# The first pair of an output projection: its products reordered, its carries bare, a store and the gate rows moved to other places

## The chip, the cores and the metric

The kernel runs on one core of a Trainium2 chip. The time is that of one execution on the device in microseconds (us); of several executions the median is given. A profile is one execution of its own, recorded by the hardware. The engines are TensorE (PE in the profile; its weight loads are PEld), VectorE (DVE), ScalarE (ACT), GpSimd (POOL) and SyncE (SP). Each takes its instructions in a fixed order. SP, ACT and POOL also issue transfers (DMA), each through a queue of its own.

## The reference

One layer of a streaming encoder over 2048 prompt frames and 32 frames of a running stream, each of width 1024. Cut to what matters here:

```python
proj = rmsnorm(h, g_mix) @ w_in                  # 1024 -> 3072, six parts
yA   = b * causal_conv3(c * h_in) * silu(zA)     # 512 wide
yB   = pooled_mix(v) * silu(zB)                  # 512 wide
h    = h + concat([yA, yB]) @ w_out              # the stage that is changed
gate = sigmoid(rmsnorm(h, g_ple) @ w_ple_gate)
h    = h + (p @ w_ple) * gate                    # p @ w_ple: the "embedding"
out  = rmsnorm(h, g_final)
```

All is float32. Two states of the mixers are outputs too.

## The kernel before

A float32 product is made of three TensorE products: each operand is split (`split`, L76) into a high part, rounded by ScalarE, and a low part, the difference, by VectorE; high by high, high by low and low by high are added up in PSUM. A tile of frames has 128 rows; `tiles` numbers 16 of them and a last one of 32.

The stages follow each other: the input projection and the mixers, in blocks of 416 columns, which write their result y to memory (`y_d`); the embedding of the first three tiles (`EARLY`, run at the end of that stage by `embedding[1](c)`); the w_out stage; the embedding of the rest; the gate stage; the final norm. The embedding's results go to memory (`e_d`) and are read in the gate stage.

The w_out stage takes the tiles in pairs. For a pair, the left matrix has two halves in rows (the two tiles) and two in columns (the two halves of y), and so has w_out; `seven` (L200) makes the block product from seven half products in place of eight (a Strassen-Winograd scheme). Sums and differences of blocks of y are made by `frame_parts` (L167): S1 to S4 beside the plain 11, 12 and 22. Those of w_out are T1 to T4; T1, T2, T3 and T4 of w_out are ready when the stage begins, 11 is too (`layout(["11"])`, from `tops`). The blocks 21 and 22 come from the bottom half of w_out, four row blocks of 512 KB (`bots`, tile `wo_q`), whose loads SP issues at the start of the stage; `rest` (L1162) splits them: ScalarE's casts make the high parts (`wo_c` for 21, `wo_d` for 22), VectorE's subtractions the low ones (`wo_d`; three tiles, d0 to d2, have this name in the profile).

A product of seven has four steps of k, with three matmuls each: twelve matmuls. Three PSUM banks take them: X (`x_o`), Y (`y_o`) and Z (`z_o`). X goes on to add to what it holds; so a `carry` first copies what it holds so far, and the next product into X waits for that copy. `carry` and `out` come from `h_ops` (L1093): a carry adds the rows of h that the result is added to (`x`) while it copies, on VectorE; a bare one is a plain copy on ScalarE, and VectorE adds it to the rows of `x` later.

The first pair (i = 0) has an order of its own (`t1_first`): S1·T1 into Z, with a bare carry; 11·11 into X, carry; S2·T2 into X, carry; S3·T3 into X, out; 12·21 into Y, out (`late`); S4·22 into Z, out; 22·T4 into X, out. The other pairs start with 11·11 and have S1·T1 between S2·T2 and S3·T3. `between` holds steps that are called between the products.

w_ple_gate, scaled by g_ple, is prepared in this stage too: `scale_gate(k)` (L1131) loads 128 rows through POOL's queue into two tiles `gs`; the function that it returns scales them on ScalarE and stores them to `g_d` through ScalarE's queue. One such block is loaded ahead of the first pair; after each pair it is scaled and stored, and the next is loaded.

The order on each engine is not that of the source: a planner goes over the instructions of a stage and gives each engine a fixed list, keeping what depends on each other in order. A tile of a ring waits for the last reader of the tile that had its place; so tiles of the w_out stage also wait for work and transfers of the stage before, whose places they take.

Of the kernel before, what the change touches and what calls it, by code (L numbers as in the profile page):

```python
# [15 lines left out]
P = 128  # L16
# [18 lines left out]
def trunk(ctx, tc, x_p, x_s, c_conv, c_pool, p_p, p_s, g_mix, w_in, conv_w, conv_b, pool_w,  # L35
# [63 lines left out]
    def embed(todo, wp, ring, queue=nc.sync):  # L99

        got = {}

        def prep(c):
            if c in got or c >= len(todo):
                return
            i = todo[c]
            r, n = tiles[i]  # L110
            if c % 4 == 0:
                pt = ring("p", i)
                m = min(4, len(todo) - c)
                full = [j for j in todo[c:c + m] if j < NT - 1]
                if full:
                    nc.sync.dma_start(pt.rearrange("p (a d) -> p a d", a=4)[:, :len(full)],
                                      p_p[r:r + len(full) * P].rearrange("(a p) d -> p a d", p=P))
                if len(full) < m:
                    nc.sync.dma_start(pt[:DEC, len(full) * PLE:(len(full) + 1) * PLE], p_s)
                got["p"] = pt  # L120
            pt = got["p"][:, (c % 4) * PLE:(c % 4 + 1) * PLE]
            pps = ring("pps", i)
            ptp = tbank(f"ptp_{i}")
            for k in range(2):
                nc.tensor.transpose(ptp[:, k * P:k * P + n], pt[:n, k * P:(k + 1) * P], ident[:n, :n])
            v = ptp.rearrange("p (k t) -> p k t", k=4)[:, :2, :n]
            split(pps[:, 0, :, :n], pps[:, 1, :, :n], v)
            got[c] = pps

        def run(c):  # L130
            i = todo[c]
            r, n = tiles[i]
            prep(c)
            prep(c + 1)
            prep(c + 2)
            pps = got[c]
            o = ring("out", i)
            for nh in range(2):
                cs = slice(nh * NH, nh * NH + NH)
                ps = bank(f"e_{i}_{nh}")  # L140
                for k in range(2):
                    for q, (a, b) in enumerate(((0, 0), (0, 1), (1, 0))):
                        nc.tensor.matmul(ps[:n], pps[:, a, k, :n], wp[k][b][:, cs],  # L143
                                         start=k + q == 0, stop=k == 1 and q == 2)
                nc.scalar.copy(o[:n, cs], ps[:n])
            queue.dma_start(e_d[r:r + n], o[:n])

        return prep, run

    def product(ps, lhs, w, n, start):  # L150

        for k in range(KH):
            for q, (a, b) in enumerate(((0, 0), (0, 1), (1, 0))):
                nc.tensor.matmul(ps[:n], lhs[:, k, a, :n], w[b][:, k], start=start and k + q == 0,  # L154
                                 stop=k == KH - 1 and q == 2, skip_group_check=True)

# [10 lines left out]
    def frame_parts(cmb, tmp, name, a11, a12, a21, a22, t1_first=False):  # L167
# [15 lines left out]
        s1 = comb("S1", a21, a22, ALU.add)  # L183
        if t1_first:
            put("S1", s1)
        put("11", a11)
        s2 = comb("S2", s1, a11, ALU.subtract)
        put("S2", s2)
        if not t1_first:
            put("S1", s1)  # L190
        put("S3", comb("S3", a11, a21, ALU.subtract))

        def more():
            put("12", a12)
            put("S4", comb("S4", a12, s2, ALU.subtract))
            return put("22", a22)

        return A, more

    def seven(name, A, W, carry, out, between={}, late=False, t1_first=False):  # L200

        step = lambda c: between[c]() if c in between else None
        X, Y, Z = (bank(f"{c}_{name}") for c in "xyz")

        def lower():
            product(Z, A["S1"], W["T1"], P, True)  # L210
            return carry(Z, (1, 1))

        if t1_first:
            c3 = lower()
        product(X, A["11"], W["11"], P, True)
        c1 = carry(X, (0, 0))
        step(1)

        def upper():
            product(Y, A["12"], W["21"], P, True)  # L220
            out(Y, c1, (0, 0))

        if not late:
            upper()
        step(2)
        product(X, A["S2"], W["T2"], P, False)
        c2 = carry(X, (0, 1))
        step(3)
        if not t1_first:
# [68 lines left out]
    with ExitStack() as s1:  # L298
# [771 lines left out]
                    early_sums(j)  # L1070

        for c in range(EARLY):
            embedding[1](c)


    with ExitStack() as s2:
# [13 lines left out]
        def half_of(x, at, n=P):  # L1090
            return x[at[0]][:n, at[1] * NH:at[1] * NH + NH]

        def h_ops(x, n, name, bare=None):  # L1093


            def carry(ps, at):
                t = st.tile([P, NH], F32, tag="t", name=f"c_{name}_{at[0]}{at[1]}")
                if at == bare:
                    nc.scalar.copy(t[:n], ps[:n])
                    return t  # L1100
                nc.vector.tensor_tensor(t[:n], ps[:n], half_of(x, at, n), op=ALU.add)  # L1101
                return t

            def out(ps, c, at):
                t = half_of(x, at, n)
                if at == bare:
# [10 lines left out]

        def prep_h(i):
            lo, hi = load_y(i, 2 * P) if i else first_y
            S[i], more = frame_parts(cmb, ss, f"y{i}", lo[:, :, :P], hi[:, :, :P], lo[:, :, P:], hi[:, :, P:], i == 0)  # L1120
            return more

        def short(name, parts, n):
# [246 lines left out]
```

## Time and profile before

| | us |
|---|---|
| median of three executions | 961.4 (960.34 to 961.96) |
| the profiled execution | 960.0 |
| its span, first to last instruction | 958.2 |
| TensorE busy in the span | 930.1 (97%) |
| VectorE, ScalarE, POOL busy | 711.9, 478.0, 133.4 |
| mean clock granted to TensorE, of 1 | 0.993 |
| first pair of the w_out stage, first matmul | 562.44 |
| second pair, first matmul | 586.04 |

The profile's lines give, for an instruction or a group: start, length, engine, line of the kernel, operation, the tile written and the tiles read, shape and count; in brackets the engine's idle time before it and what ended that time (its releaser, inferred). "ACTq", "POOLq" and "SPq" are the issuing of transfers by these engines. The chain that ended last is followed back from the last instruction to whatever released each step; an instruction off that chain could have been later at no cost. Windows are stretches of the span, with the busy time and number of instructions of PE, PEld, DVE, ACT and POOL in turn, then the granted clock of TensorE as a share of the full one, the busy share of the 16 DMA engines, and GB/s.

### The profile page before, as it was taken

The page shows a single profiled execution, that of the slowest core. Times are in us where ns is not written, and L with a number is a line of the kernel's source. Part 1 is how long each engine was busy: PE and PEld are TensorE (multiplying, and loading weights), DVE is VectorE, ACT ScalarE, POOL GpSimd, SP SyncE. Part 2 cuts the span into 40 slices and gives each one's busy share as a digit, 9 for nine tenths or more (in the row PEclk, how much of TensorE's full clock was granted, in tenths as well). Part 3 has the DMA queues.
Part 4 walks back from the last instruction along what each step waited for, and adds up shares of the span by engine and source line. Part 5 has one row for each costly group of instructions (what it writes and reads, how often), then busy time and mean ns, then how long its engine had stood idle before and what let it go on. Part 6 is the DMA issues. An engine that isn't in the chain of part 4 may idle for free.

```text
span 958.2 us, 13167 instructions
## 1 busy us (share of the span) xinstructions
PE 930.1 (97%) x4631; PEld 833.8 (87%) x4631; DVE 711.9 (74%) x1199; ACT 478.0 (50%) x883; POOL 133.4 (14%) x258
## 2 busy tenths in 40 slices
PE   7999999899999999999999989999999999999996
PEld 5999999898999999999999967888886778888883
DVE  6797987989577778585767768656645777898874
ACT  6554564644445554444544455343335775556553
POOL 3112232221001110000000011112110001112112
PEclk9999999999999999999999999999999999999998
DMA  8437696496955557337665297677676784656641
GB/s 260 123 91 216 196 282 218 153 285 218 418 155 153 152 167 212 94 114 262 189 178 171 93 285 234 193 232 228 200 197 207 259 287 133 236 188 231 226 146 49
DMA packets 132415, 190.05 MB, mean 198 GB/s; under 512 B 11708, under 2 KB 101052, under 8 KB 131069
## 3 DMA queue, kind: packets, MB, share of 16 engines
q1 hardware_dynamic: 114909, 133.67, 45.0%
q0 software_dynamic: 14704, 49.78, 15.8%
q10 hardware_dynamic: 2736, 5.77, 2.0%
q8 instruction: 36, 0.59, 0.3%
q14 instruction: 30, 0.25, 0.1%
HBM read 129.06 MB, written 60.10 MB: 197 GB/s over the span
## 4 chain that ended last, share of the span: by engine, by line
PE 69%; DMA 7%; DVE 3%; ACT 2%; issue 1%; POOL 0%; POOLq 0%; SPq 0%; ACTq 0%; DVEq 0%
PE x_g L154 9%; PE x_o L154 8%; PE x_zab L539 5%; PE z_g L154 5%; PE z_o L154 4%; PE x_ch L539 4%; PE x_zbv L539 4%; PE z_zab L539 2%; PE z_ch L539 2%; PE y_g L154 2%; DMA wg_r<-g_d 2%; PE z_zbv L539 2%; PE y_o L154 2%; PE b L539 2%; PE v L539 2%; PE zb L539 2%
## 5 line engine op out<-in xcount | busy, mean ns | idle before, releaser
L143 PE MATMUL e<-wq,pps 128*128 128x512 f32 (+1 forms) x168 | 41.8, 399 | 0.6 <-ACT pps L77 0.6
L77 ACT CAST y_S<-y_fS 128x512 fp32r<-128x512 f32 x32 | 19.6, 621 | 41.2 <-PE x_o L154 19.0
L539 PE MATMUL x_zab<-B,w_zab_S 128*128 128x416 f32 x168 | 35.9, 363 | 2.6 <-ACT V L834 1.9
L539 PE MATMUL z_ch<-B,w_ch_S 128*128 128x416 f32 x168 | 35.7, 363 | 2.6 <-ACT U L834 2.6
L154 PE MATMUL x_o<-wo_b,y_S 128*128 128x512 f32 x128 | 35.7, 391 | 0.9 <-DVE c_o L1101 0.9
L154 PE MATMUL x_g<-wg_b,g_S 128*128 128x512 f32 x128 | 36.3, 391 | 0.0
L143 PEld LDWEIGHTS e<-wq,pps 128*128 128x128 f32 (+1 forms) x168 | 29.5, 182 | 7.6 <-ACT pps L77 0.8
L374 DVE SCALAR_TENSOR_TENSOR xt<-xt,rstd_x,g_bc 128x1024 f32<-128x1024 f32 (+2 forms) x18 | 23.1, 1282 | 17.3 <-POOL rstd_x L73 16.2
L539 PEld LDWEIGHTS x_zab<-B,w_zab_S 128*128 128x128 f32 x168 | 32.3, 194 | 3.7 <-ACT V L834 2.2
L539 PEld LDWEIGHTS z_ch<-B,w_ch_S 128*128 128x128 f32 x168 | 32.5, 196 | 3.4 <-ACT U L834 3.0
L539 PE MATMUL z_zbv<-B,w_zbv_S 128*128 128x416 f32 x168 | 34.2, 352 | 0.0
L539 PE MATMUL z_zab<-B,w_zab_S 128*128 128x416 f32 x168 | 34.2, 352 | 0.0
L539 PE MATMUL x_zbv<-B,w_zbv_S 128*128 128x416 f32 x168 | 34.1, 351 | 0.0
L539 PE MATMUL x_ch<-B,w_ch_S 128*128 128x416 f32 x168 | 34.0, 351 | 0.0
L539 PEld LDWEIGHTS z_zab<-B,w_zab_S 128*128 128x128 f32 x168 | 31.7, 189 | 0.4
L1101 DVE TENSOR_TENSOR c_o<-x_o,x 128x512 f32<-128x512 f32 x16 | 11.1, 692 | 28.0 <-PE x_o L154 28.0
L539 PEld LDWEIGHTS x_ch<-B,w_ch_S 128*128 128x128 f32 x168 | 31.4, 188 | 0.3
L539 PEld LDWEIGHTS x_zbv<-B,w_zbv_S 128*128 128x128 f32 x168 | 31.3, 188 | 0.3
L539 PEld LDWEIGHTS z_zbv<-B,w_zbv_S 128*128 128x128 f32 x168 | 31.3, 188 | 0.4
L69 POOL TENSOR_SCALAR ms_f<-ssq_f 128x1 f32<-128x1 f32 x16 | 7.4, 462 | 169.8 <-ACT junk L88 169.6
L1268 DVE SCALAR_TENSOR_TENSOR h<-h,rstd_f,g_bc 128x1024 f32<-128x1024 f32 x16 | 20.6, 1284 | 12.4 <-POOL rstd_f L73 12.3
L154 PEld LDWEIGHTS x_o<-wo_b,y_S 128*128 128x128 f32 x128 | 24.0, 188 | 6.0 <-ACT y L77 1.3
(534 smaller groups left out, 2662.5 us busy)
## 6 DMA issues: line engine op xcount, KB each, us to landing
y<-y_d SPq DMA_DIRECT2D x16, 512.0 KB, 7.7
x<-in_x_prompt_dram SPq DMA_DIRECT2D x16, 512.0 KB, 7.4
h_d<-x SPq DMA_DIRECT2D x16, 512.0 KB, 2.9
h<-h_d SPq DMA_DIRECT2D x16, 512.0 KB, 3.5
e<-e_d SPq DMA_DIRECT2D x16, 512.0 KB, 5.8
out_dram<-h POOLq DMA_DIRECT2D x16, 512.0 KB, 3.1
xt<-in_x_prompt_dram SPq DMA_DIRECT2D x15, 512.0 KB, 12.4
e_d<-eout SPq DMA_DIRECT2D x13, 512.0 KB, 3.4
```

Of the source, the lines that this page charges most:

```text
L69: nc.gpsimd.tensor_scalar(ms[:n], ssq[:n], scalar1=1.0 / D, scalar2=EPS, op0=ALU.mult, op1=ALU.add)
L77: ins = nc.scalar.copy(hi, src)
L143: nc.tensor.matmul(ps[:n], pps[:, a, k, :n], wp[k][b][:, cs], start=k + q == 0, stop=k == 1 and q == 2)
L154: nc.tensor.matmul(ps[:n], lhs[:, k, a, :n], w[b][:, k], start=start and k + q == 0, stop=k == KH - 1 and q == 2, skip_group_check=True)
L374: nc.vector.scalar_tensor_tensor(xt[:n], xt[:n], r[:n], g_bc[:n], op0=ALU.mult, op1=ALU.mult)
L539: nc.tensor.matmul(ps[:, :NB], lhs[:, k, x], b[:, k, y], start=start and k + q == 0, stop=stop and k == KH - 1 and q == 2, skip_group_chec ...
L1101: nc.vector.tensor_tensor(t[:n], ps[:n], half_of(x, at, n), op=ALU.add)
L1268: nc.vector.scalar_tensor_tensor(h[:n], h[:n], rf[:n], g_bc[:n], op0=ALU.mult, op1=ALU.mult)
```

## The change

Six edits, five of them in or around the first pair.

- The last of the three early embedding tiles: its second half is copied from PSUM by VectorE instead of ScalarE, and its store is issued by POOL instead of ScalarE.
- The first pair no longer starts with S1·T1 (`t1_first` goes). It starts with 11·11; S1·T1 is cut into two halves of two k steps (six matmuls); the first half stands behind 11·11 and the second behind S2·T2 (`in_parts`).
- All three carries of the first pair are bare.
- In three products of the first pair the order of the matmuls within the product is by parts, with k inside: 11·11 takes high by high, high by low (of the weights), low by high; 12·21 and S4·22 take high by high, low (of the frames) by high, high by low (of the weights). Before, and in all other products, k is outside.
- `frame_parts` makes the high and low parts of 11 and S2 ahead of S1 for every pair.
- The gate rows: the first block is loaded behind the first pair in the source; `next_gate` scales what was loaded and loads the next block. It is called after each pair and once more within the second pair.

```diff
-        def run(c):
+        def run(c, last=False):
...
-                nc.scalar.copy(o[:n, cs], ps[:n])
-            queue.dma_start(e_d[r:r + n], o[:n])
+                (nc.vector.tensor_copy if last and nh else nc.scalar.copy)(o[:n, cs], ps[:n])
+            (nc.gpsimd if last else queue).dma_start(e_d[r:r + n], o[:n])
...
-    def product(ps, lhs, w, n, start):
-        for k in range(KH):
-            for q, (a, b) in enumerate(((0, 0), (0, 1), (1, 0))):
+    FINE = (0, 0), (0, 1), (1, 0)
+    def product(ps, lhs, w, n, start, ks=range(KH), order=None):
+        if order is not None:
+            steps = [(k, *p) for p in order for k in ks]
+            for i, (k, a, b) in enumerate(steps):
+                nc.tensor.matmul(ps[:n], lhs[:, k, a, :n], w[b][:, k], start=start and i == 0, stop=i == len(steps) - 1,
+                                 skip_group_check=True)
+            return
+        for k in ks:
+            for q, (a, b) in enumerate(FINE):
...
-    def seven(name, A, W, carry, out, between={}, late=False, t1_first=False):
+    def seven(name, A, W, carry, out, between={}, late=False, in_parts=False):
+        frames_late, weights_late = (FINE, FINE[::2] + FINE[1:2]) if in_parts else (None, None)
-        def lower():
-            product(Z, A["S1"], W["T1"], P, True)
-            return carry(Z, (1, 1))
-        if t1_first:
-            c3 = lower()
-        product(X, A["11"], W["11"], P, True)
+        def lower(*parts):
+            for ks in parts:
+                product(Z, A["S1"], W["T1"], P, ks.start == 0, ks)
+            return carry(Z, (1, 1)) if ks.stop == KH else None
+        parts = range(KH // 2), range(KH // 2, KH)
+        product(X, A["11"], W["11"], P, True, order=frames_late)
...
-            product(Y, A["12"], W["21"], P, True)
+            product(Y, A["12"], W["21"], P, True, order=weights_late)
...
+        if in_parts:
+            lower(parts[0])
         step(2)
         product(X, A["S2"], W["T2"], P, False)
         c2 = carry(X, (0, 1))
         step(3)
-        if not t1_first:
-            c3 = lower()
+        c3 = lower(parts[1]) if in_parts else lower(range(KH))
...
-        product(Z, A["S4"], W["22"], P, False)
+        product(Z, A["S4"], W["22"], P, False, order=weights_late)
...
-            embedding[1](c)
+            embedding[1](c, c == EARLY - 1)
...
-                if at == bare:
+                if bare and at != (1, 0):
...
-        rest_gate = scale_gate(0)
+        gate_rows = iter(range(KC))
+        waiting = []
+        def next_gate():
+            for rest_gate in waiting:
+                rest_gate()
+            waiting[:] = [scale_gate(k) for k in [next(gate_rows, None)] if k is not None]
...
-            seven(f"o{i}", S.pop(i), W, *h_ops(x, P, f"o{i}", None if i else (1, 1)), {1: rest} if i == 0 else {}, True, i == 0)
+            seven(f"o{i}", S.pop(i), W, *h_ops(x, P, f"o{i}", i == 0), {0: {1: rest}, 2: {3: next_gate}}.get(i, {}), True, i == 0)
...
-            rest_gate()
-            if i + 2 < NT - 1:
-                rest_gate = scale_gate(i // 2 + 1)
+            next_gate()
```

More of the change, by code (lines that the diff above doesn't have):

```diff
@@ L165, in weight_sums, with frame_parts @@
             split(W[q][0][:, k], W[q][1][:, k], t)
-    def frame_parts(cmb, tmp, name, a11, a12, a21, a22, t1_first=False):
+    def frame_parts(cmb, tmp, name, a11, a12, a21, a22):
         A = {}
@@ L183, in frame_parts @@
         s1 = comb("S1", a21, a22, ALU.add)
-        if t1_first:
-            put("S1", s1)
         put("11", a11)
@@ L188, in frame_parts @@
         put("S2", s2)
-        if not t1_first:
-            put("S1", s1)
+        put("S1", s1)
         put("S3", comb("S3", a11, a21, ALU.subtract))
@@ L198, in frame_parts @@
         return A, more
-    def seven(name, A, W, carry, out, between={}, late=False, t1_first=False):
+    def seven(name, A, W, carry, out, between={}, late=False, in_parts=False):
         step = lambda c: between[c]() if c in between else None
+        frames_late, weights_late = (FINE, FINE[::2] + FINE[1:2]) if in_parts else (None, None)
         X, Y, Z = (bank(f"{c}_{name}") for c in "xyz")
-        def lower():
-            product(Z, A["S1"], W["T1"], P, True)
-            return carry(Z, (1, 1))
-        if t1_first:
-            c3 = lower()
-        product(X, A["11"], W["11"], P, True)
+        def lower(*parts):
[4 more added lines that the diff above has]
+        product(X, A["11"], W["11"], P, True, order=frames_late)
         c1 = carry(X, (0, 0))
@@ L228, in seven @@
         step(3)
-        if not t1_first:
-            c3 = lower()
+        c3 = lower(parts[1]) if in_parts else lower(range(KH))
         step(4)
@@ L1091, in half_of, with h_ops @@
             return x[at[0]][:n, at[1] * NH:at[1] * NH + NH]
-        def h_ops(x, n, name, bare=None):
+        def h_ops(x, n, name, bare=False):
             def carry(ps, at):
                 t = st.tile([P, NH], F32, tag="t", name=f"c_{name}_{at[0]}{at[1]}")
-                if at == bare:
+                if bare and at != (1, 0):
                     nc.scalar.copy(t[:n], ps[:n])
@@ L1105, in out @@
                 t = half_of(x, at, n)
-                if at == bare:
+                if bare and at != (1, 0):
                     nc.vector.tensor_tensor(t, t, c[:n], op=ALU.add)
@@ L1119, in prep_h @@
             lo, hi = load_y(i, 2 * P) if i else first_y
-            S[i], more = frame_parts(cmb, ss, f"y{i}", lo[:, :, :P], hi[:, :, :P], lo[:, :, P:], hi[:, :, P:], i == 0)
+            S[i], more = frame_parts(cmb, ss, f"y{i}", lo[:, :, :P], hi[:, :, :P], lo[:, :, P:], hi[:, :, P:])
             return more
```

## The prediction

> **What bounds the kernel now.** I read the page first, then the chain that ended last, TensorE's waits around the first w_out pair, the timelines of its engines there, and last the granted clock. The page's first part and the chain (start, length, what):
>
> ```profile
> PE 930.1 (97%) x4631; PEld 833.8 (87%) x4631; DVE 711.9 (74%) x1199; ACT 478.0 (50%) x883; POOL 133.4 (14%) x258
> ```
>
> ```profile
> 555.87 7.08 DMA y<-y_d
> 562.97 15.63 DMA wo_q<-in_w_out_dram
> 580.75 2.73 PE z_o L154 x12
> 583.48 5.44 PE x_o L154 x24
> ```
>
> TensorE is the bound (97%), but not here: before 580.75 the chain runs through a load, the fourth bottom row block of w_out, issued at 562.97 when a y load had landed. The pair's products ahead of y_o are off the chain. One matmul takes 5.44/24 = 0.227 us of TensorE's time. What TensorE waits for between 540 and 590 us (sum, times, longest):
>
> ```profile
> PE x_o L154 <- DVE c_o L1101: 1.8, 2, 0.9
> PE z_o L154 <- ACT y_S L77: 1.7, 1, 1.7
> PE y_o L154 <- ACT wo_c L77: 0.8, 1, 0.8
> PE y_o L154 <- DVE wo_d L78: 0.2, 1, 0.2
> ```
>
> 4.5 us stand idle. The first two lines are what the change goes for; only the last two are on the chain. TensorE's timeline (start, length, instruction, idle before):
>
> ```profile
> 552.08 8.67 PE L143 MATMUL e<-wp,pps 128*128 128x512 f32 x36
> 562.44 3.31 PE L154 MATMUL z_o<-wo_a,y_S 128*128 128x512 f32 x12 [1.69 <-ACT y_S L77]
> ...
> 573.19 2.96 PE L154 MATMUL x_o<-wo_b,y_S 128*128 128x512 f32 x12 [0.88 <-DVE c_o L1101]
> 576.00 0.39 PE L154 MATMUL y_o<-wo_c,y 128*128 128x512 f32 x1
> ...
> 579.29 0.49 PE L154 MATMUL y_o<-wo_c,y 128*128 128x512 f32 x1 [0.84 <-ACT wo_c L77]
> ...
> 580.35 0.40 PE L154 MATMUL y_o<-wo_c,y 128*128 128x512 f32 x1
> 580.59 2.89 PE L154 MATMUL z_o<-wo_d,y_S 128*128 128x512 f32 x12
> ...
> 586.04 2.88 PE L154 MATMUL x_o<-wo_c,y 128*128 128x512 f32 x12
> ```
>
> And ScalarE's, where the three wo_c casts end their wait on a load:
>
> ```profile
> 559.38 0.59 ACT L145 COPY eout<-e 128x512 f32<-128x512 f32 x1 [0.82 <-PE e L143]
> ...
> 561.40 0.33 ACTq L146 DMA_DIRECT2D e_d<-eout  x1
> 561.77 0.62 ACT L77 CAST y_S<-y_fS 128x512 fp32r<-128x512 f32 x1 [0.40 <-ACT eout L145]
> ...
> 574.69 0.62 ACT L77 CAST wo_c<-wo_q 128x512 fp32r<-128x512 f32 x1 [0.62 <-DMA wo_q<-in_w_out_dram]
> ...
> 576.32 0.62 ACT L77 CAST wo_c<-wo_q 128x512 fp32r<-128x512 f32 x1 [0.48 <-DMA wo_q<-in_w_out_dram]
> ...
> 578.62 0.62 ACT L77 CAST wo_c<-wo_q 128x512 fp32r<-128x512 f32 x1 [1.16 <-DMA wo_q<-in_w_out_dram]
> ```
>
> The second to fourth block of the weights land at 574.7, 576.3 and 578.6. Why not sooner: this stretch's row ends with the granted clock, the busy share of the DMA engines and GB/s.
>
> ```profile
> 570.00:574.00 4.00, 3.12 (x15) 2.29 (x14) 2.25 (x4) 1.59 (x3) 0.00 (x0) 1.00 1.06 238
> ```
>
> All 16 DMA engines are full (1.06): the loads wait for their turn, not for their issue.
>
> **The change, part by part.** Start: the last embedding tile's second half is copied by VectorE and its store issued by POOL, so ScalarE, free at 559.38 + 0.59, casts y_11 by about 560.6, and x_o follows the embedding's last matmul at about 560.6 in place of 562.44: 1.8 us gained. VectorE's copy, 0.69 us by its rows for this shape below, is covered by its idle 4.54 us: it starts behind the embedding's last matmul (552.08 + 8.67 = 560.75), and y's low part behind it is ready at 560.8 + 2 x 0.69 = 562.2, wanted eight matmuls after 560.6, at 562.4. Uncovered, it would cost its 0.7. Bare carries with half of S1·T1 behind each: 6 x 0.227 = 1.36 us of filler over a copy of 0.59, behind one cast of 0.62 in the second case: both waits of 0.88 go. So S3·T3's 48th matmul is issued at 560.6 + 48 x 0.227 = 571.5 instead of 576.0: 4.5 us earlier.
>
> ```profile
> 562.42 0.69 DVE L78 TENSOR_TENSOR y_S<-y_fS,y_S 128x512 fp32r<-128x512 f32 x1 [4.54 <-ACT y_S L77]
> ...
> 574.27 0.68 DVE L78 TENSOR_TENSOR wo_d<-wo_q,wo_d 128x512 fp32r<-128x512 f32 x1
> ...
> 579.27 0.69 DVE L78 TENSOR_TENSOR wo_d<-wo_q,wo_c 128x512 fp32r<-128x512 f32 x1 [1.01 <-ACT wo_c L77]
> ```
>
> What is late next: y_o. Its weights still land until 578.6, so the 4.5 us become one long wait, from 571.5 to 579.29. Worth: nothing.
>
> Late parts last: in front of the last cast k was outermost, and behind 579.29 three matmuls of y_o stood, ending in 580.59 - 579.29 = 1.30 us with VectorE's wait. Now the order is high by high for all k, then y's low parts, then the weights' low parts: behind the last cast stand 1 + 4 + 4 = 9 matmuls, 9 x 0.227 = 2.04 us. Loss: 0.74 us. The order helps only where low parts are late; here the high part is.
>
> The clock: windows of 3.41 us, with TensorE's busy time in the first bracketed pair and the granted clock third from the end, then one product on either side of the second pause:
>
> ```profile
> 169.79:173.20 3.41, 0.95 (x4) 0.60 (x5) 3.41 (x7) 1.72 (x3) 0.85 (x1) 1.00 0.92 272
> 173.20:176.61 3.41, 3.41 (x11) 3.26 (x10) 3.41 (x6) 0.98 (x2) 0.00 (x0) 0.50 0.39 129
> ...
> 214.16:217.57 3.41, 1.04 (x6) 0.70 (x4) 3.41 (x8) 1.09 (x2) 0.54 (x1) 1.00 1.11 320
> 217.57:220.99 3.42, 3.17 (x9) 3.04 (x10) 3.42 (x7) 1.86 (x4) 0.00 (x0) 0.50 0.24 84
> ...
> 558.90:562.32 3.42, 1.85 (x8) 1.14 (x7) 0.00 (x0) 1.72 (x4) 0.55 (x1) 1.00 0.99 301
> ```
>
> ```profile
> 212.78 2.43 PE L539 MATMUL x_ch<-B,w_ch_S 128*128 128x416 f32 x12
> 217.82 3.97 PE L539 MATMUL z_ch<-B,w_ch_S 128*128 128x416 f32 x12 [2.62 <-ACT U L834]
> ```
>
> A window with 28 to 30% work (0.95 and 1.04 of 3.41) is followed by one at half clock; a window with 54% (1.85 of 3.42) is not. 12 matmuls then took 3.97 for 2.43: 1.54 us lost. Today's idle is spread thin enough. After the change the wait holds four matmuls of 0.4 us in some 7.8 us, so that a whole window in it has a quarter of work or less: the clock is halved when the 33 matmuls y_o (9), z_o (12) and x_o (12) begin. It stays so for the rest of that window, plus a whole one if the rest filled too little of it; between 30 and 54% I take 42%. So 0.42 x 3.41 = 1.4 us at least, 1.42 x 3.41 = 4.8 at most, by where the window happens to stand, 3.1 in the mean. At 1.54/3.41 us per us that is 0.6 to 2.2, in the mean 1.4 us. [...]
>
> The Trainium skill, TensorE: Matmul & The Clock Gate, "HAM oscillation", asks only that no TensorE idle gap exceed about 3.4 us. The trace is harsher: a gap of 2.62 us sufficed. By the page nearly nothing would be lost, as matmuls break the wait into gaps of at most 3.4, and the sum would be 0.7 us.
>
> The transfers: this store moves from ScalarE's queue to POOL's, in the order built ahead of the first two gate loads; all move through the same engines. The gate loads, though written later, are built directly behind it, ahead of POOL's first rstd work: they move by the 0.7 us of one issue. Their share of the DMA time between 560 and 580, and issue to landing:
>
> ```profile
> q0 software_dynamic: 544, 0.53, 11.1%
> ```
>
> ```profile
> gs<-in_w_ple_gate_dram POOLq DMA_DIRECT2D x2, 256.0 KB, 14.2
> ```
>
> ```profile
> 561.77 1.44 POOL L1139 DMA_DIRECT2D gs<-in_w_ple_gate_dram  x2 [6.69 <-ACT eout L145]
> ```
>
> If they left the stretch wholly, the weights gain 11.1% of 20 = 2.2 us; if the store and they crowd in earlier, the weights lose about the issue's 0.7. I take 0, being nearest to the built order. SP's queue: the fourth block's issue now waits on another transfer, in time by 561.77, 1.2 us sooner; with full engines, 0.
>
> From the second pair on: gate scaling and squares change places on ScalarE, and some low parts and adds on VectorE, beside TensorE's work. The first gate row is scaled in the second pair, the last as before behind the last pair. TensorE's waits from 586 us to the end:
>
> ```profile
> PE pth L1229 <- DVE pps L78: 1.8, 2, 1.4
> PE e L143 <- ACT pps L77: 0.6, 1, 0.6
> PE ptp L125 <- DVE pps L78: 0.4, 1, 0.4
> ```
>
> None is on a carry or a gate row, so the eight pairs cover all of this: taken 0; with the cover gone one misplaced instruction costs its 0.6 to 0.7. For the same reason a pair that starts late ends late: nothing behind it gives the time back.
>
> Sum: 0.74 + 1.4 = 2.1 us. The profiled run took 960.0 (span 958.2), so 962.1; it lay 1.4 under the median 961.4, so **963.5 us**.
>
> **The rivals.** First, the weights bind but the clock holds: only the 0.74 stays, 960.0 + 0.74 + 1.4 = 962.1. For it: the wait is broken by matmuls; against it: the two windows above. (The Trainium skill's TensorE: Matmul & The Clock Gate, "HAM oscillation", would lead here.)
>
> Second, on the other side: the four loads land earlier, because gate rows and store get out of their way. At 2.2 us earlier the result is 2.1 - 2.2: 961.3, no change. It turns into a gain of 0.2% where they land 2.7 us earlier and the wait, then 5 us with matmuls in it, keeps the clock: 0.74 - 2.7, 959.4; with the earlier issue in full, 2.2 + 1.2 = 3.4, it is 958.7. Against it: full engines, and the built order.
> Third, slower: POOL's store lands late. The first wo_d low part (574.27) writes where its tile lies and waits for it, and all later low parts queue behind on VectorE. Like the gate loads' 14.2 us, it would land at 575.7, still harmless; six low parts of 0.6 must run before 579.3, so from 576 on each us costs one. At 579: 3 more, 966.5.
>
> **How the numbers follow.** Forecast 0.60 (own range 962.3 to 964.7: clock 0.6 to 2.2, weights 0.5 either way); clock holds 0.12; weights earlier 0.20, half of it beyond 0.2%; store late 0.08. 0.2%, 1.9 us, is about what a measurement of this kernel can tell. Of the forecast some 7 in 10 lie above 963.3: slower 0.42 + 0.08 = 0.50; same 0.18 + 0.12 + 0.10 = 0.40; faster 0.10. The range runs from 960.3, within the earlier weights, to 965.2, into the late store.
>
> **What would show it.** Right: x_o first and near 560.6; no wait on c_o; waits of y_o on wo_c of some 6 us in all; a granted clock of 0.5 in a window around 580; nine matmuls of y_o behind the last cast; the second pair's start, 586.04 before, late by the sum. Wrong: wo_c casts well ahead of 578.6 on the pair's own time, the clock at 1.0 throughout, or VectorE waiting for e_d.

## The result, and the profile after

The changed kernel takes 964.3 us (median of 12 executions, 962.1 to 968.4) beside 961.7 us for the kernel before in the same job (960.3 to 963.4): a ratio of 1.0035 with an interval of 1.0023 to 1.0048, slower by some 3 us. The profiled execution took 964.3 us, its span is 962.5 us. The page's first part shows the same work as before, within the noise:

```profile
PE 931.8 (97%) x4631; PEld 835.5 (87%) x4631; DVE 712.8 (74%) x1200; ACT 478.3 (50%) x884; POOL 134.8 (14%) x259
```

Executions differ by microseconds ahead of the changed stage: the first matmul of the early embedding stands at 551.82 in one of the profiled runs below and at 557.49 in another. So times below are also given on the stage's own clock, counted from that matmul: 552.08 in the run of before, 553.84 here. On it the second pair starts at 586.04 - 552.08 = 33.96 before and at 590.74 - 553.84 = 36.90 after. The stage lost 2.94 us; from there to the end of the span it is 372.2 us before and 371.8 after. The whole loss lies in the first pair.

TensorE's timeline of the changed kernel (start, length, instruction, idle before):

```profile
553.84 8.67 PE L143 MATMUL e<-wp,pps 128*128 128x512 f32 x36
562.35 3.00 PE L160 MATMUL x_o<-wo_c,y 128*128 128x512 f32 x12
...
570.66 3.01 PE L165 MATMUL x_o<-wo_b,y_S 128*128 128x512 f32 x12
573.52 0.39 PE L160 MATMUL y_o<-wo_c,y 128*128 128x512 f32 x1
574.39 0.49 PE L160 MATMUL y_o<-wo_c,y 128*128 128x512 f32 x1 [0.49 <-ACT wo_c L77]
578.31 0.51 PE L160 MATMUL y_o<-wo_c,y 128*128 128x512 f32 x1 [3.43 <-ACT wo_c L77]
581.04 2.50 PE L160 MATMUL y_o<-wo_c,y 128*128 128x512 f32 x5 [2.23 <-ACT wo_c L77]
583.34 1.91 PE L160 MATMUL y_o<-wo_d,y 128*128 128x512 f32 x4
585.05 3.13 PE L160 MATMUL z_o<-wo_d,y_S 128*128 128x512 f32 x12
...
590.74 2.88 PE L165 MATMUL x_o<-wo_c,y 128*128 128x512 f32 x12
```

The pair now starts 8.51 us after the embedding's first matmul instead of 10.36, no wait on a carry is left, and 12·21 begins at 19.68 instead of 23.92: 4.2 us earlier. All of it, and a little more, stands in front of y_o's matmuls. TensorE's waits between 540 and 590 us are one line now:

```profile
PE y_o L160 <- ACT wo_c L77: 6.1, 3, 3.4
```

(The three waits are 0.49, 3.43 and 2.23 us in the timeline.) The weights did not move. ScalarE's four casts of the bottom blocks:

```profile
571.72 0.62 ACT L77 CAST wo_c<-wo_q 128x512 fp32r<-128x512 f32 x1 [0.21 <-DMA wo_q<-in_w_out_dram]
...
573.72 0.62 ACT L77 CAST wo_c<-wo_q 128x512 fp32r<-128x512 f32 x1 [0.86 <-DMA wo_q<-in_w_out_dram]
...
577.64 0.62 ACT L77 CAST wo_c<-wo_q 128x512 fp32r<-128x512 f32 x1 [2.78 <-DMA wo_q<-in_w_out_dram]
...
580.37 0.62 ACT L77 CAST wo_c<-wo_q 128x512 fp32r<-128x512 f32 x1 [1.59 <-DMA wo_q<-in_w_out_dram]
```

The last stands at 580.37 - 553.84 = 26.53, before at 578.62 - 552.08 = 26.54. The chain that ended last says the same in its way (start, length, what):

```profile
557.54 5.51 DMA e_d<-eout
563.07 17.28 DMA wo_q<-in_w_out_dram
581.04 4.21 PE y_o L160 x9
```

The fourth block was issued 1.7 us earlier on the stage's clock (563.07 - 553.84 = 9.23 for 562.97 - 552.08 = 10.89) and then took 17.28 us to land instead of 15.63. And the chain goes through nine matmuls of y_o, that is from the last cast on, where before only the last two of y_o stood on it.

Windows of 3.41 us on the grid of the clock (busy time of PE, PEld, DVE, ACT, POOL, then granted clock, DMA share, GB/s):

```profile
571.85:575.27 3.42, 2.55 (x11) 1.54 (x9) 2.91 (x6) 2.15 (x4) 0.00 (x0) 1.00 1.05 256
575.27:578.68 3.41, 0.37 (x1) 0.19 (x1) 0.78 (x2) 1.04 (x2) 0.00 (x0) 1.00 1.12 236
578.68:582.09 3.41, 1.19 (x4) 0.85 (x4) 1.97 (x4) 1.82 (x5) 0.00 (x0) 0.50 0.71 194
582.09:585.51 3.42, 3.42 (x10) 2.65 (x9) 1.05 (x3) 2.20 (x5) 0.00 (x0) 0.50 0.04 13
585.51:588.92 3.41, 3.41 (x16) 2.80 (x15) 2.97 (x6) 0.40 (x1) 0.00 (x0) 1.00 0.15 17
```

A window with 11% work (0.37 of 3.41) is followed by one at half clock; that one, filled only from 581.04 on (35%), by a second. TensorE's weight loads are slower there too: 188 ns each from 563 to 569, 322 to 330 from 581 to 585.4. From the matmul that waited for the last cast (581.04) to the second pair stand 33 matmuls and 9.70 us; at 0.227 us each they take 7.48. The clock cost 2.2 us, and it was half for 585.51 - 581.04 = 4.47 us of that time. Before, it was 586.04 - 579.29 = 6.75 us from the same point. So the 2.95 us lost behind it are 0.73 for the order (7.48 - 6.75) and 2.2 for the clock.

### The profile page after: what moved, and what is told of

The parts are those of the page before. It is cut to its first block, busy times and chain, and to the rows that moved or that the text cites. A ratio compares the mean times of both kernels' runs of the same rounds, so it can differ in the third digit from the quotient of the medians.

```text
span 962.5 us, 13162 instructions
## 1 busy us (share of the span) xinstructions
PE 931.8 (97%) x4631; PEld 835.5 (87%) x4631; DVE 712.8 (74%) x1200; ACT 478.3 (50%) x884; POOL 134.8 (14%) x259
## 4 chain that ended last, share of the span: by engine, by line
PE 71%; DMA 6%; DVE 2%; ACT 1%; issue 1%; POOL 0%; POOLq 0%; ACTq 0%; DVEq 0%
PE x_g L165 9%; PE x_o L165 8%; PE x_zab L550 5%; PE z_g L165 5%; PE x_ch L550 4%; PE x_zbv L550 4%; PE z_o L165 4%; PE z_zab L550 2%; PE z_ch L550 2%; PE y_g L165 2%; PE z_zbv L550 2%; PE y_o L165 2%; PE za L550 2%; PE b L550 2%; PE c L550 2%; PE v L550 2%
```

## The experiments

Theory: the landing of the last w_out block sets the time; behind it stand the matmuls that the order leaves, and the halved clock; what is saved ahead of it is worth nothing. Rivals: the slow matmuls have another cause than the wait; the new order is free; the store or the gate rows in their new places cost; the savings count.

The stage's clock in every profiled run (us from the embedding's first matmul; "behind" is the second minus the first column), and the ratio to the kernel before:

| kernel | last wo_c cast | second pair | behind | ratio, interval |
|---|---|---|---|---|
| before | 26.54 | 33.96 | 7.4 | 1 |
| changed | 26.53 | 36.90 | 10.4 | 1.0035 (1.0023 to 1.0048) |
| e1_k_outer | 26.54 | 35.51 | 9.0 | 1.0024 (1.0010 to 1.0039) |
| e2_busy | 26.91 | 35.19 | 8.3 | 1.0019 (1.0000 to 1.0037) |
| e3_late_last_alone | 26.44 | 34.51 | 8.1 | 1.0015 (0.9999 to 1.0032) |
| e4_busy_k_outer | 25.90 | 33.33 | 7.4 | 1.0012 (1.0002 to 1.0023) |
| f4_store_back | 25.99 | 36.51 | 10.5 | 1.0043 (1.0027 to 1.0059) |
| f1_x_behind | 21.67 | 29.95 | 8.3 | 0.9956 (0.9941 to 0.9971) |
| f2_gate_behind | 20.89 | 29.17 | 8.3 | 1.0027 (1.0012 to 1.0042) |
| f3_weights_first | 20.69 | 28.59 | 7.9 | 1.0055 (1.0041 to 1.0068) |
| g1_gate_late_twice | 20.65 | 28.56 | 7.9 | 1.0011 (0.9993 to 1.0029) |
| g6_gate_late_by_parts | 20.65 | 28.96 | 8.3 | 1.0009 (0.9992 to 1.0027) |
| g2_before_x_behind | 23.99 | 32.09 | 8.1 | 0.9983 (0.9966 to 0.9999) |
| g3_x_behind_k_outer | 20.65 | 28.55 | 7.9 | 0.9938 (0.9914 to 0.9961) |

The intervals are 0.1 to 0.2% wide on either side; where a question is worth less than that, the stage's clock decides. That is one profile for each kernel: the last cast stands between 25.90 and 26.91 in the first seven rows, in which no load was moved by itself, so a difference of half a microsecond in the second column says little; the third, counted from the cast, is steadier.

**The clock.** Work for TensorE is put into the wait, nothing else is changed:

```diff
         out(X, c3, (1, 1))
-        step(5)
+        if 5 in between:
+            between[5](A)
...
+        def busy(A, n=24):
+            ps = tbank("busy")
+            for c in range(n):
+                k, (a, b) = c % KH, FINE[c // KH % 3]
+                nc.tensor.matmul(ps, A["S3"][:, k, a], W["T3"][b][:, k], start=c == 0, stop=c == n - 1, ...)
```

> The changed kernel with 24 more matmuls of 128x512 between S3·T3 and 12·21, into a PSUM bank that nobody reads (added work of 24 x 0.227 = 5.4 us of TensorE's time, all inside the wait of some 6 us); they compute nothing that is used. Theory (the idle wait halves the clock): the clock stays at 1.0 around 580, the second pair starts some 34.7 us after the embedding's first product instead of 36.9, and the time falls by about 2.2 us against the changed kernel: ratio to the kernel before 1.0008 to 1.0012. Rival (the slow matmuls behind the wait have another cause, such as the shared memory ports or the weight loads): no gain, ratio 1.0035, or worse by what of the 5.4 us sticks out.

TensorE's timeline of this kernel:

```profile
574.83 5.38 PE L1194 MATMUL busy<-wo_b,y_S 128*128 128x512 f32 x23
580.04 0.84 PE L160 MATMUL y_o<-wo_c,y 128*128 128x512 f32 x3
582.54 1.43 PE L160 MATMUL y_o<-wo_c,y 128*128 128x512 f32 x5 [1.66 <-ACT wo_c L77]
...
590.15 2.88 PE L165 MATMUL x_o<-wo_c,y 128*128 128x512 f32 x12
```

5.4 us of useless work make the stage 1.7 us faster, though the last cast came 0.4 us later. From the waiting matmul on it is 590.15 - 582.54 = 7.61 us for the same 33 matmuls, not 9.70: 2.1 us were the clock, which stays at 1.0 in this stretch. The rival (another cause behind the wait) falls. In the whole time, 1.0019 for 1.0035, the intervals overlap; it is the trace that shows it.

**The order.** It is undone in the changed kernel, and done alone in the kernel before:

```diff
-        frames_late, weights_late = (FINE, FINE[::2] + FINE[1:2]) if in_parts else (None, None)
+        frames_late, weights_late = (FINE, None) if in_parts else (None, None)
```

> The changed kernel with the matmuls of 12·21 and S4·22 again with k outermost (late parts no longer last); all else as changed. Theory (the landing of the last w_out block sets the time, 0.7 us of the loss is order, 2.2 us is the halved clock): three matmuls instead of nine stand behind the last wo_c cast, so the second pair starts 0.7 us earlier than in the changed kernel, 36.2 us after the embedding's first product instead of 36.9; with nine instead of four matmuls inside the wait the clock may also be halved for one window less (another 1.1 us). Ratio to the kernel before 1.0015 to 1.0028. Rival (the order costs nothing, all of the loss is clock or lies elsewhere): ratio 1.0035 as measured for the change.

```diff
-            product(Y, A["12"], W["21"], P, True)
+            product(Y, A["12"], W["21"], P, True, t1_first)   # by parts, late parts last
...
-        product(Z, A["S4"], W["22"], P, False)
+        product(Z, A["S4"], W["22"], P, False, t1_first)
```

> The kernel before with one part of the change alone: the matmuls of 12·21 and S4·22 of the first pair by parts, late parts last. Theory: nine matmuls instead of three behind the last cast: the second pair starts 0.7 us later (34.7 instead of 34.0 us after the embedding's first product), ratio 1.0007; if the matmuls now missing in the wait from 576 to 579 leave a window with less than 30 per cent of work, up to 1.5 us more, ratio up to 1.0023. Rival (the order is free, or helps as the low parts are late): ratio 1.0000 or below.

Alone, the order costs 34.51 - 33.96 = 0.55 us of the stage with the last cast 0.1 us earlier: behind the cast 8.07 for 7.42, 0.65 us. The clock has no part in that: the run's one window of half clock in this stage lies ahead of 12·21. TensorE's timeline, behind a short wait:

```profile
584.57 1.42 PE L154 MATMUL y_o<-wo_c,y 128*128 128x512 f32 x5 [0.54 <-ACT wo_c L77]
...
591.97 2.88 PE L160 MATMUL x_o<-wo_c,y 128*128 128x512 f32 x12
```

Undone in the changed kernel, it gives 1.4 us: the order's 0.7, and less time at half clock behind the last cast. The wait still halved the clock for two windows, but the second ended 30.9 us after the embedding's first matmul instead of 31.7. Beside the 7.4 us behind the last cast of the kernel before, 1.55 us are left for the clock (8.97 - 7.42) in place of 2.2.

**Both mends.** The 24 matmuls and k outermost together:

> Both mends together: the changed kernel with k outermost in 12·21 and S4·22 and with the 24 unused matmuls in the wait. Theory: what is left of the change is the earlier start and the carries, which lie ahead of the landing of the weights and are worth nothing: second pair 34.0 us after the embedding's first product, as before, ratio 1.0000 (0.9993 to 1.0007). Rival (the 4.5 us saved ahead of 12·21 do count once the clock holds): ratio down to 0.996. Second rival (something behind the first pair, as the gate rows' new places, costs too): ratio over 1.001.

```profile
576.99 5.60 PE L1194 MATMUL busy<-wo_b,y_S 128*128 128x512 f32 x24
...
590.64 2.88 PE L165 MATMUL x_o<-wo_c,y 128*128 128x512 f32 x12
```

The useless work is 5.4 us, more than the 4.2 that the change saves ahead of 12·21, and the stage takes no longer than before: 33.33 us, 7.43 behind the last cast for 7.42. In this run the cast came 0.6 us earlier than in the others, and TensorE ran without a wait from y_o's first matmul (25.12) on; so this run shows that order and clock were the whole loss, and that the savings were not counted in it, but not by itself what they are worth. The next run does. The ratio, 1.0012 with an interval from 1.0002, lies above the expected range and just over the 1.001 of the second rival (something behind the first pair costs too), which the interval neither shows nor excludes. What the profiled run has behind the first pair is a wait of 1.0 us on a carry in the second pair, since the added work made the planner put only 4 matmuls of S1·T1 ahead of S2·T2 there instead of 10. That is a side effect of this experiment; the changed kernel has no such wait.

**The store.** One part undone: copy and store on ScalarE again.

```diff
-            embedding[1](c, c == EARLY - 1)
+            embedding[1](c)
```

> The changed kernel with one part undone: the last early embedding's second half copied by ScalarE again and its store on ScalarE's queue. Theory (off the path): the pair's first matmul 10.4 us after the embedding's first product instead of 8.5, the wait of 12·21 shorter by as much, the last cast at 26.5 as now; second pair 36.9, or 35.8 if the shorter wait halves the clock for one window less; ratio 1.0020 to 1.0035. Rival (the store on POOL's queue slows the weights): cast earlier than 26 and ratio under 1.002. Second rival (the earlier start is worth its 1.8 us): ratio 1.005.

The pair starts 1.9 us later again (10.38), 12·21 at 21.57, and the second pair at 36.51: the 1.9 us come out of the wait (3.7 us in place of 6.1) and not out of the time. The cast came 0.5 us earlier, as far as runs differ anyway; counted from it, the second pair stands at 10.5 us for 10.4. So the earlier start is worth nothing here, and the store's place costs nothing that shows. The first rival falls by both of its signs together (the cast at 25.99, but the ratio 1.0043); the second falls by the stage's clock alone: the ratio is above the expected range, and its interval holds the 1.005 of that rival. The timeline and the windows of this run tell something more:

```profile
577.49 0.50 PE L160 MATMUL y_o<-wo_c,y 128*128 128x512 f32 x1 [1.29 <-ACT wo_c L77]
579.94 2.50 PE L160 MATMUL y_o<-wo_c,y 128*128 128x512 f32 x5 [1.95 <-ACT wo_c L77]
```

```profile
574.48:577.89 3.41, 1.65 (x6) 0.66 (x4) 2.42 (x5) 2.21 (x4) 0.00 (x0) 1.00 1.09 281
577.89:581.30 3.41, 1.46 (x4) 1.16 (x4) 2.25 (x5) 2.10 (x5) 0.00 (x0) 0.50 0.59 183
```

No gap is longer than 1.95 us, and a window with 48% work (1.65 of 3.41) was followed by half clock. An earlier window of this run, from 560.83 on, has 50% (1.71 of 3.41) and was not.

**The weights earlier.** Two ways to take transfers out of the stretch, each alone. First, SP issues the second pair's rows of h behind the four blocks:

```diff
-            load_bottom(k, bots[k])
+            last_bottom = load_bottom(k, bots[k])        # load_bottom returns its instruction
...
-            x = [load_rows(xh, "x", i + b, x_p) for b in range(2)] if i else [first_x, second_x]
+            if i:
+                with tc.issue_after(last_bottom.ins):
+                    x = [load_rows(xh, "x", i + b, x_p) for b in range(2)]
+            else:
+                x = [first_x, second_x]
```

> The changed kernel with the loads of the second pair's rows of h (two x tiles, 1 MB) issued by SP behind the four w_out blocks instead of ahead of them; no other order changes. Theory (the blocks' landing sets the time, and the loads only wait for their turn at full engines): 1 MB at the 240 GB/s of this stretch is 4.3 us; the last wo_c cast comes up to 4.3 us earlier than 26.5 us after the embedding's first product, and the second pair starts at 31 to 34 us instead of 36.9, ratio to the kernel before 0.997 to 1.0005. Rival (the last block's landing hangs on something else, as the place that it waits for or on how the packets take turns): cast at 26, second pair 36 to 37, ratio 1.0035. Second rival: the x tiles now land late and the second pair waits for them instead.

Second, POOL issues the gate rows' loads behind the rstd work of the pair (`powers` collects the instructions of L73):

```diff
-            next_gate()
+            with tc.issue_after(powers[-1].ins):
+                next_gate()
```

> The changed kernel with the loads of the gate rows really put behind the first pair: POOL issues them behind the rstd work of each pair's second tile. Theory (0.5 MB less at full engines): the last cast comes up to 2.2 us earlier, the second pair at 34.5 to 36.9 us after the embedding's first product, ratio 1.001 to 1.0035. Rival (POOL's transfers take their share beside the others without slowing them): no change of the cast, 26.5, and ratio 1.0035.

Both move the wall. With the x loads out of the way the last cast comes at 21.67 and the stage ends 7.0 us earlier than in the changed kernel, more than expected (29.95, for 31 to 34); the ratio is 0.9956, faster than the kernel before. Of the cast's 4.9 us, 2.4 are an earlier issue (the fourth block at 6.8 on the stage's clock for 9.2) and 2.4 a shorter way to landing (14.84 us for 17.28); the edit does both and doesn't tell them apart. Behind this cast the clock holds. With the gate rows out of the way the cast comes at 20.89, 5.6 us earlier, where at most 2.2 had been expected for 0.5 MB; the fourth block was issued at 8.7 and landed after 12.19 us. (The ratio, 1.0027, fell into the expected range by luck: the stage gained far more, and the second pair lost it again, as is shown below.) The transfers of 5 us of each run, from 17 us on the stage's clock, tell why; first the changed kernel (570.84 to 575.84), then the one with the gate rows behind (573.28 to 578.28); the queue's line gives packets, MB and share of the engines:

```profile
DMA packets 684, 1.34 MB, mean 269 GB/s; under 512 B 305, under 2 KB 374, under 8 KB 684
q1 hardware_dynamic: 345, 1.06, 81.1%
q0 software_dynamic: 339, 0.28, 26.7%
```

```profile
DMA packets 1146, 1.94 MB, mean 389 GB/s; under 512 B 59, under 2 KB 876, under 8 KB 1146
q1 hardware_dynamic: 1145, 1.94, 104.3%
```

With POOL's gate loads in flight (q0) the queue of the weights (q1) has 81% of the engines and moves 1.06 MB, 1.3 MB for a full share; without them it has all and moves 1.94. The gate rows take a quarter of the engines and slow what the others carry. The two stretches don't carry the same (the second has more packets of 1 KB), but like compared with like says it more plainly: by the packets' own times in the two traces, a 4096-byte packet of SP's queue takes 242 ns in the mean in the first stretch and 159 in the second. The price of the gate rows is more than their share of the time. It is not always paid, though. In the kernel before, from 566 to 569 us, gate rows were in flight beside SP's loads and ScalarE's store, and such a packet took 160 ns; once the store was through (570 to 574) it took 281:

```profile
DMA packets 487, 1.23 MB, mean 410 GB/s; under 512 B 187, under 2 KB 187, under 8 KB 487
q0 software_dynamic: 179, 0.11, 11.9%
```

What it takes besides the gate rows stays open. (The Trainium skill, DMA: Bandwidth & Descriptors, "Specifications", gives 512 B as the least transfer at full rate. That rule does not account for it here: 305 of the 684 packets are under 512 B, but their own time is 5 of the 80 us that 16 engines have in 5 us, and it is the 4096-byte packets that got slower. What these small packets carry was not looked into.)

But moving the gate rows lost all it had gained, in the second pair, which takes 24.75 us for 19.21 in the changed kernel: ScalarE waits 10.29 us there for a gate row whose load was issued only at 589.2, and TensorE for ScalarE. TensorE's line of f2_gate_behind with the idle time before it:

```profile
606.12 4.28 PE L167 MATMUL x_o<-wo_T,y 128*128 128x512 f32 x12 [3.98 <-ACT y L79]
```

**All of it, and the late gate rows.** Both moves and k outermost:

> The changed kernel with three things: the x loads of the second pair behind the four w_out blocks, the gate rows' loads behind the first pair, and k outermost again in 12·21 and S4·22. Theory: with 1.5 MB fewer in the way the last cast comes some 5 us earlier, at 20 to 23 us after the embedding's first product; the wait of 12·21 is then 1 to 3 us instead of 6, the clock holds, and the earlier start and carries of the change are worth something at last: second pair at 27.5 to 30.5 us, ratio 0.9935 to 0.9965. Rival: as for the two edits alone, cast at 26, ratio 1.0020 to 1.0030.

The first pair did as expected, 28.59, and the whole became the slowest of all. ScalarE's timeline, then TensorE's:

```profile
594.76 0.72 ACT L1156 ACTIVATE gs<-gs,vec 128x512 f32<-128x512 f32 x1 [6.17 <-DMA gs<-in_w_ple_gate_dram]
...
598.72 0.72 ACT L1156 ACTIVATE gs<-gs,vec 128x512 f32<-128x512 f32 x1 [3.24 <-DMA gs<-in_w_ple_gate_dram]
```

```profile
601.33 5.49 PE L167 MATMUL x_o<-wo_b,y_S 128*128 128x512 f32 x12 [7.84 <-DVE c_o L1114]
```

The gate row that the changed kernel scales within the second pair is now loaded only at its start; ScalarE stands in its fixed order before a load that has not landed, with the casts of the pair behind it. TensorE waits 7.84 us and comes back at half clock. So the scaling was moved on, with all else as here:

```diff
-{0: {1: rest}, 2: {3: next_gate}}
+{0: {1: rest}, 8: {3: next_gate}}
```

> The kernel with the weights first (x loads of the second pair behind the w_out blocks, gate rows' loads behind the first pair, k outermost in 12·21 and S4·22), and the extra scaling of a gate row moved from the second pair to the fifth. Theory (that kernel lost its gain because ScalarE waited 6.2 us for a gate row loaded only at 588, with the casts of the second pair queued behind): no such wait, second pair still 28.6 us after the embedding's first product, 5.4 us earlier than before; ratio 0.9935 to 0.9955. Rival (the late gate loads cost wherever they are scaled, by contention with the y loads): a wait of TensorE on y parts in the second or third pair, ratio over 0.998.

The second pair is clean, but neither side had it right: the wait went along to the fifth pair, where one row is again scaled just behind the issue of its load. ScalarE and TensorE there:

```profile
657.83 0.72 ACT L1156 ACTIVATE gs<-gs,vec 128x512 f32<-128x512 f32 x1 [10.68 <-DMA gs<-in_w_ple_gate_dram]
```

```profile
661.76 5.46 PE L167 MATMUL z_o<-wo_d,y_S 128*128 128x512 f32 x12 [4.22 <-ACT y L79]
```

The same kernel with the late parts last, as changed:

> The kernel with the weights first and the extra scaling of a gate row in the fifth pair, but with the late parts last in 12·21 and S4·22, as changed. Theory: the casts come at the pace of ScalarE, 1.04 us apart, the last at 20.7; nine matmuls behind it instead of three, second pair at 29.0 to 29.2 us instead of 28.6, ratio 0.0005 above that of the kernel with k outermost. Rival (low parts late, so that late parts last pays here): 28.6 us or less, ratio the same or lower.

28.96 for 28.56 in the stage: 0.4 us for the order, where the casts come at ScalarE's own pace, 1.04 us apart. The ratios of the two don't tell them apart. A version that scales no row in the pair that loads it was not tried.

**Do the savings count once the weights are early?** The x loads behind the blocks, in the kernel before:

> The kernel before with one thing: the x loads of the second pair behind the w_out blocks. Theory (what the change saves ahead of 12·21 is worth nothing while the weights are late, and counts once they are early): the last cast at some 22 us after the embedding's first product, TensorE is then the limit; 12·21 begins at 23.9 as before and the second pair at 23.9 + 36 x 0.227 = 32.1 us, 1.9 us earlier than before and 2.2 later than the changed kernel with the same edit (29.9); ratio 0.9975 to 0.9985. Rival (the change is worth nothing even then): 29.9 us, ratio 0.9956.

```profile
577.15 0.39 PE L154 MATMUL y_o<-wo_c,y 128*128 128x512 f32 x1
...
585.31 2.88 PE L154 MATMUL x_o<-wo_c,y 128*128 128x512 f32 x12
```

Second pair at 585.31 - 553.22 = 32.09, the 32.1 expected: TensorE runs through from 577.15 on. The changed kernel with the same edit stands at 29.95. There the change is worth 2.1 us, with the very same parts that were worth nothing above. And with k outermost as well:

> The changed kernel with the x loads of the second pair behind the w_out blocks, and k outermost again in 12·21 and S4·22; the gate rows as changed. Theory (the last cast at 21.7 still ends a wait, so six matmuls fewer behind it count, 0.7 us, less what VectorE's low parts are late): second pair at 29.2 to 29.5 us after the embedding's first product instead of 29.9; ratio 0.9948 to 0.9953. Rival (without a long wait the order is free, or the low parts are what is late, as the edit was meant): 29.9 or more, ratio 0.9956 or more.

```profile
571.82 0.39 PE L165 MATMUL y_o<-wo_c,y 128*128 128x512 f32 x1
...
574.02 0.50 PE L165 MATMUL y_o<-wo_d,y 128*128 128x512 f32 x1 [0.23 <-DVE wo_d L78]
...
580.73 2.88 PE L165 MATMUL x_o<-wo_c,y 128*128 128x512 f32 x12
```

A wait of 0.23 us is all that is left of the stage's. 28.55 us is 5.4 less than before, and 1.4 less than with the x loads alone where 0.4 to 0.7 were expected: 1.0 of it is the last cast, which came at 20.65 for 21.67 with the same order of loads, so the order's own part is 0.4; 957.6 us against 962.3 in the same job, ratio 0.9938 (0.9914 to 0.9961). This version beats both kernels.

## Why the prediction was right

963.5 us were forecast and 964.3 measured; the mechanism is the forecast one, and the sum is 0.8 us short in the stage (2.1 for 2.94). The short term is the clock's.

- What bounds the kernel: right. The last cast stands at 26.53 for 26.54, and moving it (f1, g3) is what moved the time.
- Start and carries, "worth nothing": right. 4.2 us saved of the 4.5 forecast, all turned into the wait of y_o, 6.1 us (some 6 forecast). With the start 1.9 us later again (f4_store_back) the second pair came no later, 36.51 for 36.90.
- Late parts last, 0.74: right; 0.73 by the trace, 0.65 alone in the kernel before, 0.4 where the casts come early.
- The clock, 0.6 to 2.2 with 1.4 in the mean: the mechanism right, the size at the upper end, 2.2 in the profiled run and 2.1 by the experiment. Two steps of the term are mis-sized. The first is "between 30 and 54% I take 42%". It decides whether a half-clock window is followed by a second one, but 30 and 54% come from windows at full clock. At half clock a higher share is needed to end it, as the window behind the wait in e1_k_outer shows:

```profile
576.06:579.47 3.41, 2.21 (x4) 1.07 (x4) 1.62 (x3) 2.12 (x4) 0.00 (x0) 0.50 0.97 230
579.47:582.89 3.42, 3.21 (x7) 2.15 (x7) 1.75 (x4) 3.24 (x7) 0.00 (x0) 0.50 0.15 50
```

  TensorE was busy 65% of the first (2.21 of 3.41), and the second is at half clock too. In e4_busy_k_outer, far ahead of this stage (175.57 to 178.98), 70% was not enough either; the emptiest half-clock window in these traces (from 60 us on) that was followed by full clock has 83% (2.83 of 3.41, e1_k_outer from 173.29 on). A matmul takes twice as long at half clock (five of y_o in 2.30 us from 581.04 on, 0.46 us each for 0.227), so 70 to 83% busy is the work of 35 to 42% of a full-clock window: the 42% would fit as a share of work, and was used as a share of time. That is a reading of these rows; no run varies it by itself. With 70 to 83% in place of 42% the prediction's own working gives 1.2 to 1.3 windows in the mean, 4.1 to 4.5 us at half clock instead of 3.1. The second step is the rate. "1.54/3.41" divides by a whole window, but that product began at 217.82, 0.25 us into the window: 1.54/3.17 = 0.49, nearly the half that the clock says. Together the mean is 2.0 to 2.3 us, as measured. In the profiled run itself the first window was only 35% full, so 42% would have led to the same 4.47 us; that this run stands above the mean of 3.1 is also where the window happened to stand, which is luck. (The Trainium skill's rule in TensorE: Matmul & The Clock Gate, "HAM oscillation", no idle gap over about 3.4 us, led to the rival in which the clock holds. The changed kernel's longest gap, 3.43 us, doesn't decide on it; the gaps of at most 1.95 us of f4_store_back speak against it.)
- The transfers, 0: right for this change, since the gate loads and the store do not leave the stretch. But the price of the second rival, "11.1% of 20 = 2.2 us" if they left it wholly, was wrong: 5.6 us. A share of engine time was taken for the whole cost, and the packets beside the gate rows got slower as well; so the point of 2.7 us at which that rival turns into a gain was nearer than it seemed.
- POOL's store late: did not happen. It was issued at 563.79 and landed after 7.6 us, at 571.4.
- From the second pair on, nothing: right, 371.8 us to the end for 372.2. How thin that cover is, the late gate rows showed. The order of the parts in 11·11 and the earlier 11 and S2 in `frame_parts` were not tried by themselves.

## What to carry to other kernels

Look first for what ends last in a stage: time saved ahead of a late load becomes a wait, and waiting that stands close together can cost more than the same idle time spread out, because the clock can be halved behind it (4.5 us spread out before cost no clock here, 3.7 us close together in f4_store_back did). Move the load first (what stands ahead of it in its queue and is needed later, and what slows the engines beside it); the same savings then count. Before moving a load later, look for the instruction that reads it: on an engine with a fixed order, everything behind that reader waits too.

## What was not expected of the hardware

- A window about half full can halve the clock, with no gap above 1.95 us in it or beside it: 48% was followed by half clock in f4_store_back and 50% in e3_late_last_alone (first row below). But this profile's busy time gives no sharp bound. A window with 44% in f2_gate_behind (second row) was followed by one at full clock (third row), one with 51% in g2_before_x_behind (171.11 to 174.53) by one at half.

```profile
565.74:569.15 3.41, 1.72 (x7) 0.81 (x6) 1.34 (x3) 2.58 (x5) 1.44 (x2) 1.00 1.02 308
600.65:604.06 3.41, 1.50 (x7) 0.92 (x5) 1.19 (x2) 2.43 (x5) 0.68 (x1) 1.00 0.45 166
604.06:607.47 3.41, 1.35 (x6) 1.17 (x7) 3.41 (x7) 1.14 (x2) 0.68 (x1) 1.00 0.35 93
```

- A half-clock window is prolonged more easily than its busy share suggests: those in which TensorE was busy 35 to 70% of the time were each followed by another.
- Useless matmuls can make a kernel faster: 5.4 us of them gave back 1.7 us of the stage.
- One queue's transfers can slow the others by more than their share: with the gate rows in flight the engines moved 269 GB/s, without them 389, all of them busy in both, and a 4096-byte packet took 242 ns for 159. Beside a store of ScalarE's queue this did not show.
